# mLSTM heads: state steps and scores on the projections' PSUM tiles, the head's steps moved later, row sums later, Fourier stage in background steps

## The chip, the cores and the metric

One Trainium2 chip, one core of it. The time is device microseconds of one execution of the whole program. TensorE (PE) multiplies matrices into PSUM tiles, with its weight loads on a track of their own (PEld); VectorE (DVE) and ScalarE (ACT) read PSUM and work element by element; GpSimd (POOL) and SyncE (SP) mostly issue DMA transfers. Each engine works its instructions off in the order in which the compiled program holds them.

## The reference, cut to what matters

One layer of a diffusion backbone: 1024 latent tokens and 256 context tokens, 1024 channels, float32. Half a SwiGLU feed-forward, then token mixing (a 2-D Fourier transform of one channel group beside a bidirectional chunkwise mLSTM of 4 heads with 256 channels), then another half feed-forward.

```python
def ada_params(cvec, w, b):
    m = jax.nn.silu(cvec) @ w + b          # 9 x 1024 columns: shift, scale, gate of each sub-layer
...
    qk = jax.nn.silu(dwconv(p[..., COL_Q:COL_V], conv_w, conv_b))    # convolution over 3 tokens
...
# mLSTM, one direction, one chunk of 128 tokens
        w = jnp.exp(dmat - m_t[..., None])                            # decay inside the chunk
        s = jnp.einsum("bhtd,bhsd->bhts", qx, kx) * w                 # scores
        num = a[..., None] * jnp.einsum("bhtd,bhde->bhte", qx, C) + jnp.einsum("bhts,bhse->bhte", s, vx)
        den = a * jnp.einsum("bhtd,bhd->bht", qx, n) + jnp.sum(s, axis=-1)
        h = num / jnp.maximum(jnp.abs(den), jnp.exp(-m_t))[..., None]
        C_new = decay[..., None, None] * C + jnp.einsum("bhsd,bhse->bhde", kx * wk[..., None], vx)
...
        return h_f + flip(h_b)                                        # both directions
    y = jnp.fft.fftn(z, axes=(1, 2, 4), norm="ortho").real            # the Fourier half
```

## The kernel before

**Projections.** Every large matrix product goes through `mm3` (L153): three 128x512 matmuls, one each for the high and the low part of the split operands, so a projection of 128 output channels (`feat_major`) is 24 matmuls for each of the two halves of 512 tokens. The float32 weights `wr` come by DMA, ACT casts them to `wh` (L140) and DVE forms the rest `wl` (L141). Results go to PSUM tiles with the tag "mm" (4 of them). Small work uses two other PSUM tags: "aux" (4) and "qc" (for the products of q with the states).

**Background steps.** Code that must run beside the projections is written as Python generators. Before every three matmuls the projection calls `tick(1/16)`; `tick` adds `rate/16` to a credit, at most 8, and takes one step of the generator at the head of the queue for each whole credit (a second, separate generator, `side`, has its own rate). While no generator is queued the credit still grows, so a newly queued one starts with up to 8 steps at once. The compiled program's order within an engine is found by a scheduler after that and can differ from the order of the Python calls.

**A head.** For each of the 4 heads the program runs the projections of k (two of 128 channels, k0 and k1), then of q (q0, q1), then a few gate projections. `qk_proj` evicts each projection to a row with margins (ACT, L1259), and `conv` forms the convolution over three tokens and its SiLU (DVE L979, L980, L981, ACT L983, DVE L984), for each half of the tokens. `mlstm_head` runs as the background generator beside the q and gate projections:

- *State phase*, chunks 7 down to 1: `tokens` turns the k of a chunk from channel-major to token-major (PE transposes L1292 into an aux tile, ACT copy L1293), `state_keys` scales it (ACT, L1141), `state_step` multiplies with v into two aux tiles (L1149) and adds to the decayed state (DVE, L1154). All 8 backward states are kept.
- *Main loop*, chunks 0 to 7: `weights(c)` fetches the decay rows (DMA `m<-r_l`), adds the mask (DVE L1320), takes the exponential (ACT L1322), multiplies q by k into an aux tile `S` (L1325) and S by the decay (DVE L1328), multiplies q by the two states (L1334), advances the forward state (L1149, L1154) and forms the combined score matrix (DVE L1347, L1348). `turn(c)` transposes this (PE L1357, ACT L1358) one step later, `values(c)` multiplies it by v (L1364) and normalises (DVE L1368, which waits for POOL's part of the square root), `store(c)` transposes the result (L1375) and writes it out.

**Other work around it.** The row sums of the modulation (`ada_rest`): for one half of 1024 columns, eight DMAs of 128x512 into "ld" (or other) tiles, each multiplied and added by DVE (L251, L253) into an accumulator; ACT and DVE split it, PE sums over partitions with a selector matrix (L264), and `ada_cols` turns the row (L277). In the heads this is the `side` generator from head 1 on; the scheduler may set its instructions earlier. The Fourier stage `fourier_rest` is a plain call after q1 of head 0: its PE work (L1469, L1477) runs in one piece on mm tiles. `ctx_project` makes the keys and states of the context tokens before head 0, with the same `state_step`.

Of the kernel before, what the change touches and what calls it, by code (L numbers as in the profile page):

```python
# [13 lines left out]
ALU = mybir.AluOpType  # L14
# [20 lines left out]
class Kernel:  # L35
# [203 lines left out]
    def ada_rest(self, streams, chunks, tags=("wa", "u", "u", "b"), halves=(0, 1), lag=0):  # L239
        nc = self.nc  # L240
        w = self.a["w_ada"][0]
        for ch in chunks:
            for hf in halves:
                acc = {s: self.s512(tags[1]) for s in streams}
                for k in range(ND):
                    t = self.s512(tags[0])
                    nc.sync.dma_start(t, w[k * P : (k + 1) * P, ch * D + hf * TB : ch * D + (hf + 1) * TB])
                    yield
                    for s in streams:
# [5 lines left out]
                yield  # L255
                for s in streams:
                    ah, al = self.s512(tags[2], F32R), self.s512(tags[2], F32R)
                    self.split_act(ah, al, acc[s])
                    if s == streams[0]:
                        pr = self.aux()  # L260
                    for _ in range(1 + lag):
                        yield
                    for i, part in enumerate((ah, al)):
                        nc.tensor.matmul(pr[:2, :], self.sel[:, s, :], part, start=s == streams[0] and i == 0,  # L264
                                         stop=s == streams[-1] and i == 1)
# [602 lines left out]
    def ffn_ctx_in(self, w13, uh, ul):  # L868
# [3 lines left out]
        for c in range(6):  # L872
# [29 lines left out]
            self.defer(lambda gt=gt, n=wid // 256: self.ctx_turn(gt, n, g))  # L902
# [253 lines left out]
    def ctx_project(self, u, gw):  # L1156
# [14 lines left out]
        def key_in(f, c, raw):  # L1171
# [10 lines left out]
            self.defer(lambda: key_out(ct, kf), 2.0)  # L1182
# [9 lines left out]
        for c in range(2):  # L1192
# [7 lines left out]
            for f in range(4):  # L1200
                self.defer(lambda f=f, c=c, raw=raw: key_in(f, c, raw), 0.5 + f)
# [28 lines left out]
    def feat_major(self, col, u2, sink):  # L1230
# [3 lines left out]
        ps = [self.mm() for _ in range(NB)]  # L1234
        for b in range(NB):
            for k in range(ND):
# [34 lines left out]
    def mlstm_head(self, h, q, k, v, gates):  # L1271
# [25 lines left out]
        kw = {}  # L1297
        tokens(NCH - 1)
# [12 lines left out]
        work = {}  # L1311

        def weights(c):
            A, B = self.s512("m"), self.s512("m")
            W = A[:, :256].rearrange("p (d s) -> p d s", d=2)
            SW = A[:, 256:512].rearrange("p (d s) -> p d s", d=2)
# [6 lines left out]
            S = self.aux()  # L1323
            for i in range(2):
                nc.tensor.matmul(S[:, :P], at(q, i, c), at(k, i, c), start=i == 0, stop=i == 1)  # L1325
            den = self.small([P, 12], "den", bufs=3)
# [12 lines left out]
            if c < NCH - 1:  # L1339
                self.state_step(kw.pop(c), va(c), db[:, h, c : c + 1], Cf, Cf)  # L1340
# [4 lines left out]
            nc.vector.tensor_tensor(sc, rd, col2(1, c), op=ALU.mult)  # L1345
            pr = B[:, :P]
            nc.vector.tensor_scalar_mul(pr, SW[:, 1, :], rd[:, 1:2])  # L1347
            nc.vector.scalar_tensor_tensor(pr, SW[:, 0, :], rd[:, 0:1], pr, op0=ALU.mult, op1=ALU.add)  # L1348
            hh = B[:, 256:512]
            nc.scalar.activation(hh, qc[0][:, :DH], AF.Copy, scale=sc[:, 0:1])  # L1350
            nc.vector.scalar_tensor_tensor(hh, qc[1][:, :DH], sc[:, 1:2], hh, op0=ALU.mult, op1=ALU.add)
            work[c] = A, B, den

        def turn(c):
            A, B, den = work[c]
# [4 lines left out]
        def values(c):  # L1360
            A, B, den = work[c]
# [4 lines left out]
            nc.scalar.activation(A[:, :DH], hh, AF.Square, accum_out=den[:, 10:11])  # L1366
# [3 lines left out]
        def store(c):  # L1370
            A, B, den = work.pop(c)
# [54 lines left out]
    def fourier_rest(self):  # L1426
# [15 lines left out]
        pt = self.mm()  # L1442
# [5 lines left out]
        pt = self.mm()  # L1448
# [369 lines left out]
```

## Time and profile before

| | us |
|---|---|
| median of 3 runs | 2721.26 (2717.82 to 2724.28) |
| the profiled execution | 2721.47 |
| its span, first to last instruction | 2719.7 |
| PE busy | 2643.7 |
| DVE busy | 1858.5 |
| ACT busy | 1104.7 |

The profiled execution stands 0.21 us above the median, and 1.8 us lie outside its span. PE is busy for 97% of the span, so the time is that of PE's matmuls plus what PE waits. A busy PE is not yet a PE at its peak: matmuls overlap, each of the 128x512 ones is reported with about 0.40 us though the next starts 0.23 us later, so waits shorter than about 0.17 us do not show as idle, and a lowered clock shows as busy time too.

### The profile page before, as it was taken

What the parts mean: (1) busy time and instruction counts of PE and PEld (TensorE: products, weight loads), DVE (VectorE), ACT (ScalarE), POOL (GpSimd) and SP (SyncE); (2) the same over time, 40 slices, a digit from 0 to 9 for tenths busy, and PEclk for the clock granted to TensorE, in tenths of its full rate; (3) what the DMA queues carried; (4) which work ended last, traced back from release to release, by engine and by line L of the source; (5) the groups of instructions that cost most, each with busy time, mean ns of one, the idle gap of its engine ahead of it and who ended that gap; (6) DMA issues with size and microseconds to landing.
All of it is one profiled execution on the core that took longest, in us unless ns stands there. A gap on an engine that the chain in (4) does not pass through costs nothing.

```text
span 2719.7 us, 34141 instructions
## 1 busy us (share of the span) xinstructions
PE 2643.7 (97%) x11657; PEld 2109.1 (78%) x11657; DVE 1858.5 (68%) x3341; ACT 1104.7 (41%) x1893; POOL 194.9 (7%) x387
## 2 busy tenths in 40 slices
PE   8899999999999999999999999999999999999998
PEld 5778888777877777777878778778887888888876
DVE  5688787899678638565364675555667887865665
ACT  4543333454455436233243333433345433334542
POOL 1111010000000001000000000000001110111000
PEclk9999999999999999999999999999999999999999
DMA  9765454868578645325223443355556654537773
GB/s 299 243 199 173 151 178 153 276 216 289 153 225 255 197 135 173 104 68 156 83 78 105 129 125 103 104 156 191 177 160 203 188 171 151 168 116 258 252 248 139
DMA packets 408990, 472.53 MB, mean 174 GB/s; under 512 B 25497, under 2 KB 256450, under 8 KB 408816
## 3 DMA queue, kind: packets, MB, share of 16 engines
q1 hardware_dynamic: 393824, 423.96, 50.3%
q0 software_dynamic: 14848, 46.33, 4.5%
q8 instruction: 92, 1.51, 0.2%
q14 instruction: 82, 0.67, 0.1%
q10 hardware_dynamic: 144, 0.07, 0.0%
HBM read 373.21 MB, written 97.04 MB: 173 GB/s over the span
## 4 chain that ended last, share of the span: by engine, by line
PE 75%; DVE 9%; DMA 8%; issue 5%; ACT 2%; SPq 1%; POOL 0%; DVEq 0%; POOLq 0%; ACTq 0%
PE mm L153 68%; DMA m<-r_l 2%; PE aux L1149 2%; DMA wr<-in_w_a_dram 2%; PE qc L1334 1%; DVE wl L141 1%; DVE u L253 1%; DMA ld<-in_w_ada_dram 1%; DMA ld<-xT 1%; DVE g L146 1%; DMA u<-in_w_ada_dram 1%; PE mm L234 1%; DMA ld<-h 0%; ACT wh L140 0%; DVE wl L146 0%
## 5 line engine op out<-in xcount | busy, mean ns | idle before, releaser
L153 PE MATMUL mm<-g,wh 128*128 128x512 f32 (+1 forms) x2552 | 827.8, 404 | 4.9 <-ACT wh L145 2.8
L153 PEld LDWEIGHTS mm<-g,wh 128*128 128x128 f32 (+1 forms) x2552 | 477.4, 189 | 108.1 <-ACT wh L145 3.7
L153 PE MATMUL mm<-g,wl 128*128 128x512 f32 (+1 forms) x1276 | 505.7, 398 | 1.6 <-DVE wl L146 1.6
L153 PE MATMUL mm<-g,o 128*128 128x512 f32 x2112 | 497.6, 395 | 0.0
L153 PEld LDWEIGHTS mm<-g,o 128*128 128x128 f32 x2112 | 397.6, 188 | 93.0
L141 DVE TENSOR_TENSOR wl<-wr,wh 128x1024 fp32r<-128x1024 f32 x226 | 278.0, 1231 | 190.4 <-ACT wh L140 189.7
L140 ACT CAST wh<-wr 128x1024 fp32r<-128x1024 f32 x226 | 236.2, 1046 | 331.7 <-PE mm L153 274.8
L153 PE MATMUL mm<-wh,g 128*128 128x512 f32 x1032 | 332.6, 399 | 2.7 <-DVE rs_t L311 1.4
L153 PEld LDWEIGHTS mm<-g,wl 128*128 128x128 f32 (+1 forms) x1276 | 240.7, 189 | 55.5 <-DVE wl L146 3.5
L153 PE MATMUL mm<-u,wh 128*128 128x512 f32 (+1 forms) x848 | 269.5, 400 | 5.2 <-DVE m L706 3.5
L153 PEld LDWEIGHTS mm<-wh,g 128*128 128x128 f32 x1032 | 194.5, 188 | 49.7 <-DVE rs_t L311 1.8
L153 PE MATMUL mm<-wl,g 128*128 128x512 f32 x516 | 204.4, 396 | 0.0
L153 PEld LDWEIGHTS mm<-u,wh 128*128 128x128 f32 (+1 forms) x848 | 160.2, 191 | 44.2 <-DVE m L706 3.9
L153 PE MATMUL mm<-wh,u 128*128 128x512 f32 x544 | 179.5, 404 | 2.0 <-ACT wh L140 2.0
L153 PE MATMUL mm<-u,wl 128*128 128x512 f32 (+1 forms) x424 | 167.4, 398 | 2.8 <-DVE wl L141 2.7
L584 DVE TENSOR_TENSOR t<-mm,t 128x512 f32<-128x512 f32 x128 | 88.1, 688 | 77.2 <-PE mm L153 77.2
L146 DVE TENSOR_TENSOR g<-t,g 128x512 fp32r<-128x512 f32 x150 | 100.2, 688 | 35.1 <-ACT g L145 23.9
L153 PEld LDWEIGHTS mm<-wh,u 128*128 128x128 f32 x544 | 103.2, 190 | 24.8 <-ACT wh L140 2.4
L145 ACT CAST o<-wa 128x512 fp32r<-128x512 f32 x88 | 54.6, 621 | 160.0 <-PE mm L153 153.5
L145 ACT CAST wh<-wr 128x1024 fp32r<-128x1024 f32 (+1 forms) x72 | 62.6, 871 | 136.7 <-PE mm L153 75.8
L153 PEld LDWEIGHTS mm<-wl,g 128*128 128x128 f32 x516 | 97.3, 189 | 22.9 <-issue 0.7
L145 ACT CAST g<-t 128x512 fp32r<-128x512 f32 x150 | 88.5, 619 | 60.8 <-PE mm L153 39.3
(472 smaller groups left out, 3552.9 us busy)
## 6 DMA issues: line engine op xcount, KB each, us to landing
wr<-in_w_a_dram SPq DMA_DIRECT2D x124, 512.0 KB, 4.4
t<-gx SPq DMA_DIRECT2D x170, 256.0 KB, 3.9
wr<-in_w_in_dram SPq DMA_DIRECT2D x80, 512.0 KB, 3.8
wr<-in_w_b_dram SPq DMA_DIRECT2D x70, 512.0 KB, 4.7
gx<-m POOLq DMA_DIRECT2D x88, 256.0 KB, 3.8
gx<-t POOLq DMA_DIRECT2D x66, 256.0 KB, 3.9
ld<-in_w_ada_dram SPq DMA_DIRECT2D x64, 256.0 KB, 2.8
ld<-h SPq DMA_DIRECT2D x48, 256.0 KB, 3.9
```

The source lines that it names most:

```text
L140: nc.scalar.copy(hv, rv)
L141: nc.vector.tensor_tensor(lv, rv, hv.bitcast(F32), op=ALU.subtract)
L145: self.nc.scalar.copy(hi, src)
L146: self.nc.vector.tensor_tensor(lo, src, hi.bitcast(F32), op=ALU.subtract)
L153: mul = lambda x, y, start, stop: self.nc.tensor.matmul(out, x, y, start=start, stop=stop, skip_group_check=grown)
L234: nc.tensor.matmul(pt[:2, :], self.sc[:, k, :], t, start=k == 0, stop=k == ND - 1)
L253: nc.vector.scalar_tensor_tensor(acc[s], t, self.sc[:, k, s : s + 1], acc[s], op0=ALU.mult, op1=ALU.add)
L584: add = lambda o, x, y: nc.vector.tensor_tensor(o, x, y, op=ALU.add)
L1149: nc.tensor.matmul(pt[:, :257], kw[:, i * P : (i + 1) * P], vaug, start=True, stop=True)
L1334: nc.tensor.matmul(pt[:, :257], at(q, i, c), C[:, i * 257 : (i + 1) * 257], start=i == 0, stop=i == 1)
```

## The change

What it does, in the order of the diff:

1. `ada_rest`: sums of a half are put off by `lag` steps through a queue; both streams' sums come in one group of matmuls, after the next half has begun to load. In the feed-forward it uses four tags instead of "u" alone and lag 4; in the heads lag 3.
2. `state_step` uses mm tiles in place of aux tiles, in the heads and in `ctx_project`.
3. `feat_major` takes its second PSUM tile only when its second half begins.
4. `mlstm_head` begins with three empty steps. In the main loop the decay part of `weights` becomes `weigh`, run one chunk ahead; the scores become `scores`, with `S` in an mm tile; the forward state step comes a step after its scores; `turn` and `values` come one chunk after the scores, `store` two. The exponential's tile is freed after the scores, the "m" tag has 5 tiles in both.
5. `fourier_rest` becomes the `side` generator of head 0, with aux tiles and empty steps between its parts, and so runs beside the v, k and q projections of head 0.
6. The heads' rate is 5.6 in place of 5.0.

```diff
@@ -236,9 +236,26 @@
             nc.scalar.copy(row[:2, :], pt[:2, :])
             self.ada_cols(row, (0, 1), ch, 0)
 
-    def ada_rest(self, streams, chunks, tags=("wa", "u", "u", "b"), halves=(0, 1), lag=0):
+    def ada_rest(self, streams, chunks, tags=("wa", "u", "u", "b"), halves=(0, 1), lag=1):
+
         nc = self.nc
         w = self.a["w_ada"][0]
+        todo = deque()
+
+        def step():
+            for x in todo:
+                x[0] -= 1
+            while todo and todo[0][0] <= 0:
+                todo.popleft()[1]()
+
+        def sums(parts, ch, hf):
+            pr = self.aux()
+            for n, (s, part) in enumerate(parts):
+                nc.tensor.matmul(pr[:2, :], self.sel[:, s, :], part, start=n == 0, stop=n == len(parts) - 1)
+            row = self.s512(tags[3])
+            nc.scalar.copy(row[:2, :], pr[:2, :])
+            todo.append([lag, lambda: self.ada_cols(row, streams, ch, hf)])
+
         for ch in chunks:
             for hf in halves:
                 acc = {s: self.s512(tags[1]) for s in streams}
...
@@ -253,21 +271,17 @@
                             nc.vector.scalar_tensor_tensor(acc[s], t, self.sc[:, k, s : s + 1], acc[s],
                                                            op0=ALU.mult, op1=ALU.add)
                 yield
+                step()
+                parts = []
                 for s in streams:
                     ah, al = self.s512(tags[2], F32R), self.s512(tags[2], F32R)
                     self.split_act(ah, al, acc[s])
-                    if s == streams[0]:
-                        pr = self.aux()
-                    for _ in range(1 + lag):
-                        yield
-                    for i, part in enumerate((ah, al)):
-                        nc.tensor.matmul(pr[:2, :], self.sel[:, s, :], part, start=s == streams[0] and i == 0,
-                                         stop=s == streams[-1] and i == 1)
-                row = self.s512(tags[3])
-                nc.scalar.copy(row[:2, :], pr[:2, :])
-                for _ in range(1 + lag):
-                    yield
-                self.ada_cols(row, streams, ch, hf)
+                    parts += [(s, ah), (s, al)]
+                todo.append([lag, lambda parts=parts, ch=ch, hf=hf: sums(parts, ch, hf)])
+                del acc
+        while todo:
+            yield
+            step()
 
     def ada_cols(self, row, streams, ch, hf):
...
         for i in range(2):
-            pt = self.aux()
+            pt = self.mm()
             nc.tensor.matmul(pt[:, :257], kw[:, i * P : (i + 1) * P], vaug, start=True, stop=True)
...
         ww = self.wunit(w[:, :, col : col + P])
-        ps = [self.mm() for _ in range(NB)]
+        ps = []
         for b in range(NB):
+            ps.append(self.mm())
             for k in range(ND):
                 self.tick(1 / 16)
...
         kw = {}
+        for _ in range(3):
+            yield
         tokens(NCH - 1)
         yield
...
-        work = {}
-
-        def weights(c):
-            A, B = self.s512("m"), self.s512("m")
+        work, decay = {}, {}
+
+        def weigh(c):
+
+            A = decay[c] = self.s512("m")
             W = A[:, :256].rearrange("p (d s) -> p d s", d=2)
-            SW = A[:, 256:512].rearrange("p (d s) -> p d s", d=2)
             rv = rs.rearrange("(d h) t -> d h t", d=2)[:, h, c * P : (c + 1) * P]
             nc.sync.dma_start(W, rv.unsqueeze(0).to_broadcast([P, 2, P]))
             for d in range(2):
                 nc.vector.scalar_tensor_tensor(W[:, d, :], W[:, d, :], col(3, c, d), self.mask[:, d, :],
                                                op0=ALU.add, op1=ALU.add)
             nc.scalar.activation(A[:, :256], A[:, :256], AF.Exp)
-            S = self.aux()
+
+        def scores(c):
+            A, B = decay.pop(c), self.s512("m")
+            W = A[:, :256].rearrange("p (d s) -> p d s", d=2)
+            SW = A[:, 256:512].rearrange("p (d s) -> p d s", d=2)
+            S = self.mm()
             for i in range(2):
                 nc.tensor.matmul(S[:, :P], at(q, i, c), at(k, i, c), start=i == 0, stop=i == 1)
-            den = self.small([P, 12], "den", bufs=3)
+            den = self.small([P, 12], "den", bufs=4)
             for d in range(2):
                 nc.vector.scalar_tensor_tensor(SW[:, d, :], S[:, :P], 1.0, W[:, d, :], op0=ALU.mult, op1=ALU.mult,
                                                accum_out=den[:, d : d + 1])
...
+        weigh(0)
         while q[1] is None:
             yield
         kw[0] = self.state_keys(kt(0), col(0, 0, 0))
-        for c in range(NCH + 1):
+        for _ in range(2):
+            yield
+
+        for c in range(NCH + 2):
             if c < NCH:
-                weights(c)
+                scores(c)
                 yield
-                turn(c)
-            if c > 0:
-                store(c - 1)
-            yield
-            if c < NCH:
-                values(c)
+                if c < NCH - 1:
+                    self.state_step(kw.pop(c), va(c), db[:, h, c : c + 1], Cf, Cf)
+                if c + 1 < NCH:
+                    weigh(c + 1)
                 if c + 1 < NCH - 1:
                     kw[c + 1] = self.state_keys(kt(c + 1), col(0, c + 1, 0))
+            if 0 < c <= NCH:
+                turn(c - 1)
+            yield
+            if 0 < c <= NCH:
+                values(c - 1)
+            if c > 1:
+                store(c - 2)
+            if c < NCH:
                 yield
...
-        pt = self.mm()
+        for _ in range(2):
+            yield
...
-        self.later(self.load_x(a["ctx"][0], CTX, "c", xc, tag="u"), self.ada_rest([0, 1], [2, 3], "uuuu", lag=2),
+        self.later(self.load_x(a["ctx"][0], CTX, "c", xc, tag="u"), self.ada_rest([0, 1], [2, 3], ("wa", "u", "u", "b"), lag=4),
...
@@ -1711,11 +1749,15 @@
         v = None
         self.side_rate = 3.0
         for h in range(HEADS):
-            if h == 1:
-                self.side = self.ada_rest([0], [5, 6, 7, 8], ("ld", "acc", "rb", "b"), lag=1)
+            if h == 0:
+                self.side = self.fourier_rest()
+            elif h == 1:
+                for _ in self.side:
+                    pass
...
-            self.later(self.mlstm_head(h, q, k, v[h % 2], gates), rate=5.0)
+            self.later(self.mlstm_head(h, q, k, v[h % 2], gates), rate=5.6)
             for i in range(2):
                 q[i] = self.qk_proj(2 * h + i, u2)
-            self.rate = 5.0
-            if h == 0:
-                self.fourier_rest()
+            self.rate = 5.6
             for _ in range((len(todo) + HEADS - 1 - h) // (HEADS - h)):
                 fill()
             self.drain()
```

Three places show how it moves instructions. The first is PE at the start of head 1, from the last matmul of the projection k1 on: `u_2598` is the second half of k0, `u_2615` the second half of k1 after its convolution, `mm_2635`/`mm_2636` the first tile of q0. Before, with 28 further matmuls of q0 where the dots stand:

```order
L153 MATMUL mm_2620_11644<-g_1761_7642,wl_2618_11640 128x512
L1292 MATMUL aux_2640_11739<-ident_63,u_2598_11547 128x128
L1292 MATMUL aux_2641_11743<-ident_63,u_2598_11547 128x128
...
L153 MATMUL mm_2636_11733<-g_1763_7644,wh_2633_11728 128x512
L153 MATMUL mm_2636_11733<-g_1755_7636,wl_2634_11729 128x512
L1292 MATMUL aux_2640_11739<-ident_63,u_2615_11636 128x128
L1292 MATMUL aux_2641_11743<-ident_63,u_2615_11636 128x128
```

and in the changed kernel:

```order
L153 MATMUL mm_2621_11671<-g_1640_7069,wl_2618_11640 128x512
L1307 MATMUL aux_2639_11738<-ident_63,u_2598_11547 128x128
L1307 MATMUL aux_2640_11742<-ident_63,u_2598_11547 128x128
L1307 MATMUL aux_2639_11738<-ident_63,u_2615_11636 128x128
L1307 MATMUL aux_2640_11742<-ident_63,u_2615_11636 128x128
...
L1163 MATMUL mm_2646_11756<-u_2243_9660,kw_2641_11746 128x257
L1163 MATMUL mm_2647_11759<-u_2243_9660,kw_2641_11746 128x257
...
L1163 MATMUL mm_2657_11783<-u_2242_9659,kw_2649_11766 128x257
L1163 MATMUL mm_2658_11786<-u_2242_9659,kw_2649_11766 128x257
L153 MATMUL mm_2635_11732<-g_1691_7253,wh_2633_11728 128x512
```

The 30 matmuls of q0 that stood between the transposes of k0's half and those of k1's half now stand behind the transposes and the first three state steps. The same holds at the start of heads 0, 2 and 3 (in head 0 one state step stands ahead of q0 in place of three).

The second place is DVE at the start of head 0 in the changed kernel: the rows around the convolution of k1's second half (`wa_2372` and `wa_2373` are k1's two rows, `u_2366` the result).

```order
L1280 COPY wa_2372_10465<-wa_2373_10466 128x1
L271 SCALAR_TENSOR_TENSOR acc_2696_11947<-ld_2714_12042,sc_83,acc_2696_11947 128x512
L995 SCALAR_TENSOR_TENSOR t_2374_10473<-wa_2372_10465,cv_687,t_2374_10473 128x512
L271 SCALAR_TENSOR_TENSOR acc_2696_11947<-ld_2725_12097,sc_83,acc_2696_11947 128x512
L993 TENSOR_SCALAR t_2376_10480<-wa_2373_10466,cv_687 128x512
L998 SCALAR_TENSOR_TENSOR u_2365_10407<-t_2375_10477,t_2374_10473 128x512
L994 SCALAR_TENSOR_TENSOR t_2376_10480<-wa_2373_10466,cv_687,t_2376_10480 128x512
L995 SCALAR_TENSOR_TENSOR t_2376_10480<-wa_2373_10466,cv_687,t_2376_10480 128x512
L271 SCALAR_TENSOR_TENSOR acc_2696_11947<-ld_2731_12138,sc_83,acc_2696_11947 128x512
L998 SCALAR_TENSOR_TENSOR u_2366_10408<-t_2377_10484,t_2376_10480 128x512
```

In the kernel before, the same convolution holds no row of the row sums; the first 16 of them (two accumulators) stand there in the main loop of head 0, behind its first forward state steps. Now all 16 stand ahead of the first state step.

The third place is PE in the main loop of head 3, from chunk 1's scores (`S` is `aux_3329` before, `mm_3337` now) to the state step behind them. Before:

```order
L1325 MATMUL aux_3329_14950<-u_3215_14479,u_3288_14758 128x128
L1334 MATMUL qc_3332_14960<-o_3274_14667,u_3288_14758 128x257
L1149 MATMUL aux_3333_14964<-u_2869_12790,kw_3323_14924 128x257
L153 MATMUL mm_3309_14854<-g_1756_7637,wh_3306_14849 128x512
L153 MATMUL mm_3309_14854<-g_1764_7645,wh_3306_14849 128x512
L1149 MATMUL aux_3334_14967<-u_2869_12790,kw_3323_14924 128x257
```

and now; the first dots stand for products of q with the states, the second for 7 more projection matmuls:

```order
L1347 MATMUL mm_3337_14987<-u_3239_14550,u_3308_14818 128x128
...
L1356 MATMUL qc_3340_14997<-o_3295_14756,u_3308_14818 128x257
L153 MATMUL mm_3331_14954<-g_1639_7068,wh_3322_14900 128x512
...
L153 MATMUL mm_3346_15027<-g_1691_7253,wl_3345_15024 128x512
L1163 MATMUL mm_3347_15031<-u_2876_12812,kw_3335_14969 128x257
L1163 MATMUL mm_3348_15034<-u_2876_12812,kw_3335_14969 128x257
L1377 MATMUL aux_3351_15044<-ident_63,m_3326_14925 128x128
```

The state step stands 9 projection matmuls behind the scores in place of directly behind them, its tiles no longer follow `S` through the four aux tiles, and the transpose behind it is that of the chunk before (`m_3326`; chunk 1's own tile is `m_3336`).

More of the change, by code (lines that the diff above doesn't have):

```diff
@@ L1345, in weights @@
             nc.vector.tensor_tensor(sc, rd, col2(1, c), op=ALU.mult)
+            hh = B[:, 256:512]
+            nc.scalar.activation(hh, qc[0][:, :DH], AF.Copy, scale=sc[:, 0:1])
+            nc.vector.scalar_tensor_tensor(hh, qc[1][:, :DH], sc[:, 1:2], hh, op0=ALU.mult, op1=ALU.add)
             pr = B[:, :P]
@@ L1348, in weights @@
             nc.vector.scalar_tensor_tensor(pr, SW[:, 0, :], rd[:, 0:1], pr, op0=ALU.mult, op1=ALU.add)
[L1349 to L1352, printed above, removed]
+            work[c] = B, den
         def turn(c):
-            A, B, den = work[c]
+            B, den = work[c]
             pt = self.aux()
@@ L1360, in values @@
         def values(c):
-            A, B, den = work[c]
+            B, den = work[c]
             hh = B[:, 256:512]
@@ L1370, in store @@
         def store(c):
-            A, B, den = work.pop(c)
+            B, den = work.pop(c)
             hh = B[:, 256:512]
@@ L1441, in fourier_rest @@
         k32 = kr[:, :256].rearrange("p (a c) -> p a c", c=8)[:, :, 0]
-        pt = self.mm()
+        for _ in range(2):
+            yield
+        pt = self.aux()
         for g in range(4):
@@ L1447, in fourier_rest @@
                        pt[:, :P].rearrange("p (g i r) -> p g i r", g=4, i=2))
-        pt = self.mm()
+        for _ in range(2):
+            yield
+        pt = self.aux()
         for i in range(2):
@@ L1451, in fourier_rest @@
                              start=i == 0, stop=i == 1)
-        y32 = self.s512("wa")
+        y32 = self.small([P, 64], "y32", bufs=1)
         nc.scalar.copy(y32[:, :64], pt[:, :64])
@@ L1461, in fourier_rest @@
                 zz.append(t)
+            yield
             Y = [self.s512("acc"), self.s512("b")]
             for j2 in range(2):
-                pt = self.mm()
+                yield
+                pt = self.aux()
                 for jj in range(2):
@@ L1475, in fourier_rest @@
                         (nc.scalar.copy if i else nc.vector.tensor_copy)(dst[:, 2 * j2 + jj], pv[:, i, jj])
-            pp, pq = self.mm(), self.mm()
+            for _ in range(2):
+                yield
+            pp, pq = self.aux(), self.aux()
             nc.tensor.matmul(pp, kh[:, :P], Y[0], start=True, stop=True)
@@ L1655, in ctx_in @@
             yield from self.prenorm(self.reload(xc[0], CTX), xc[1:], CTX, 1, 0, uc)
-            yield from self.ada_rest([0, 1], [4], lag=2)
+            yield from self.ada_rest([0, 1], [4], lag=4)
         self.later(ctx_in(), rate=3.5)
@@ L1713, in run @@
         for h in range(HEADS):
-            if h == 1:
-                self.side = self.ada_rest([0], [5, 6, 7, 8], ("ld", "acc", "rb", "b"), lag=1)
+            if h == 0:
[3 more added lines that the diff above has]
+                    pass
+                self.side = self.ada_rest([0], [5, 6, 7, 8], ("ld", "acc", "rb", "b"), lag=3)
             if h % 2 == 0:
                 v = [[self.slot("u") for _ in range(4)] for _ in range(2)]
-                br = self.bias_row(C_V + h * DH)
+                br = self.bias_row(C_V + h * DH, "st")
                 for b in range(NB):
```

11 lines of the change are left out of this document (5 added, 6 removed).

## The prediction, made before the changed kernel was run

> **What bounds the kernel now.** I read the page first, then PE's waits, then the heads stretch by stretch, then the timeline of two places.
>
> ```profile
> PE 2643.7 (97%) x11657; PEld 2109.1 (78%) x11657; DVE 1858.5 (68%) x3341; ACT 1104.7 (41%) x1893; POOL 194.9 (7%) x387
> PE 75%; DVE 9%; DMA 8%; issue 5%; ACT 2%; SPq 1%; POOL 0%; DVEq 0%; POOLq 0%; ACTq 0%
> ```
>
> PE is busy 2643.7 of 2719.7 us, and the chain that ended last runs on PE for 75%. The change neither adds nor removes matmuls, so the time moves only with what PE waits and with its clock. At most 76 us of shown idle time can be won.
>
> ```profile
> PE aux L1149 <- DVE m L1328: 9.1, 6, 3.4
> PE aux L1357 <- DVE m L1348: 7.0, 5, 2.8
> PE aux L264 <- ACT u L145: 3.6, 2, 2.0
> PE aux L1375 <- DVE m L1368: 3.6, 4, 1.6
> PE mm L1477 <- DVE acc L1475: 1.3, 1, 1.3
> PE mm L1469 <- DMA ld<-z: 1.0, 3, 0.5
> ```
>
> These are PE's waits by line: total, times, longest. The heads' main loop has three: the state step waits for the scores' reader (9.1), the transposes `turn` and `store` for DVE (7.0 and 3.6): 19.7 us. Busy time by stretch agrees:
>
> ```profile
> core 0: us, PE busy (x) PEld busy (x) DVE busy (x) ACT busy (x) POOL busy (x), PEclk, DMA share, GB/s
> 500.00:710.00 210.00, 199.86 (x873) 157.69 (x873) 188.64 (x299) 97.21 (x162) 0.00 (x0) 0.99 0.75 246
> 1023.00:1089.00 66.00, 62.59 (x271) 47.42 (x271) 60.23 (x140) 44.12 (x69) 8.19 (x40) 0.97 0.59 170
> 1200.00:1234.00 34.00, 31.70 (x135) 22.45 (x133) 21.24 (x81) 10.84 (x33) 0.68 (x2) 1.00 0.42 129
> 1353.00:1373.00 20.00, 20.00 (x93) 14.48 (x92) 12.15 (x24) 10.12 (x21) 0.45 (x2) 1.00 0.10 27
> 1234.00:1319.00 85.00, 77.99 (x364) 63.81 (x363) 46.21 (x150) 26.97 (x67) 4.39 (x8) 1.00 0.48 139
> 1373.00:1475.00 102.00, 99.10 (x459) 81.26 (x458) 59.59 (x193) 38.02 (x88) 6.19 (x29) 0.98 0.36 102
> 1567.00:1668.00 101.00, 98.20 (x460) 80.07 (x459) 63.75 (x201) 37.58 (x89) 5.88 (x11) 1.00 0.40 112
> 1717.00:1821.00 104.00, 96.88 (x446) 78.14 (x445) 58.86 (x194) 41.04 (x94) 4.48 (x9) 0.98 0.45 130
> ```
>
> The last four rows are the main loops of heads 0 to 3: idle 7.0, 2.9, 2.8 and 7.1 us, 19.8 together. 1353 to 1373 is head 1's state phase: no idle time at all. 1200 to 1234 is the Fourier stage: 2.3 idle. 500 to 710 (context's feed-forward, with row sums) has 10.1 idle, 1023 to 1089 (context's keys and states) 3.4.
>
> **The change part by part.** *Main loop: gain.* The longest wait, in head 3:
>
> ```profile
> 1735.03 0.61 PE L1325 MATMUL aux<-u,u 128*128 128x128 f32 x4
> 1736.16 0.82 PE L153 MATMUL mm<-g,wh 128*128 128x512 f32 x2
> 1738.47 0.35 DVE L1320 SCALAR_TENSOR_TENSOR m<-m,cols_l,mask 128x128 f32<-128x128 f32 x1 [4.15 <-DMA m<-r_l]
> 1740.42 0.70 PE L1149 MATMUL aux<-u,kw 128*128 128x257 f32 x2 [3.44 <-DVE m L1328]
> ```
>
> The decay rows landed late, DVE's mask waited 4.15 us, the exponential and L1328 followed, and PE's second state matmul, whose aux tile holds `S` until then, waited 3.44. The change takes this apart: the decay is made a chunk ahead, the state step has mm tiles and 9 projection matmuls (9 x 0.23, the spacing of starts in the h1 rows below: 2.1 us) ahead of it, `turn` comes a chunk after its scores. What is late next is `values` behind `turn`, with again 9 matmuls over one ACT copy. I take 19 of 23 us: the 19.8 shown and some 3 in waits too short to show, less 4 that stay. Bounds: 12 (new waits on the shared mm tiles) to 23.
>
> *Fourier stage: gain.* Its 2.3 us of idle go when its pieces run among the v projection's matmuls, and about as much in the unshown gaps of 64 isolated small matmuls may stay or go; I take 3, from 1 to 5. Its DVE and ACT work stays and now runs beside the convolutions.
>
> *Start of each head: loss.* Here the order moved against the kernel. Head 1 before:
>
> ```profile
> 1353.40 0.40 PE L153 MATMUL mm<-g,wl 128*128 128x512 f32 x1
> 1353.60 1.05 ACT L140 CAST wh<-wr 128x1024 fp32r<-128x1024 f32 x1 [3.97 <-PE mm L153]
> 1353.63 0.38 PE L1292 MATMUL aux<-ident,u 128*128 128x128 f32 x2
> 1354.55 0.69 ACT L1259 ACTIVATE wa<-mm,cc 128x512 f32<-128x512 f32 x1
> 1354.68 1.23 DVE L141 TENSOR_TENSOR wl<-wr,wh 128x1024 fp32r<-128x1024 f32 x1 [3.66 <-ACT wh L140]
> 1356.00 0.75 DVE L981 SCALAR_TENSOR_TENSOR t<-wa,cv,t 128x512 f32<-128x512 f32 x1
> 1357.25 0.75 DVE L980 SCALAR_TENSOR_TENSOR t<-wa,cv,t 128x512 f32<-128x512 f32 x1
> 1359.96 0.69 DVE L984 SCALAR_TENSOR_TENSOR u<-t,t 128x512 f32<-128x512 f32 x1 [0.70 <-ACT t L983]
> 1360.74 0.41 PE L1292 MATMUL aux<-ident,u 128*128 128x128 f32 x2
> ```
>
> The last matmul of k1 starts at 1353.40. A cast that ACT began first, the eviction (L1259), DVE's weight rest (L141) and the convolution's operations follow, and its second half is written at 1360.65: 7.25 us. PE fills them with q0: between the transposes at 1353.63 and at 1360.74 lie 30 projection matmuls, 6.9 us. In the changed order these 30 stand behind the waiting transposes and the first state steps. The compiled order keeps the cast and L141 in the same places in the chain, so the cover is the last matmul's own 0.23 us and two transposes of the same kind, another 0.23: PE stands 7.25 - 0.46 = 6.8 us. The three empty steps do not help, because with 8 credits saved up they are spent at the first tick together with the five that follow. Heads 1 to 3: 3 x 6.8 = 20.4 us. Without the cast (0.95 us from end to end of it on ACT) the chain could not be under about 6.3, so the floor is 3 x 5.8 = 17.4.
>
> Behind the wait the first state steps run with little beside them: copy and scaling on ACT (0.33 and 0.52 us), then a pair of small matmuls per chunk. In head 1 before, the way from the transposes at 1360.74 to the first state matmul took 1.5 us, filled by projections; now it is bare, less the seven transposes now done there, so about 1 us per head is lost. Against this stands a row of PE's weight loads:
>
> ```profile
> PEld aux L1292 <- DVE o L1154: 5.4, 17, 0.3
> ```
>
> These 5.4 us (aux tiles that wait for the state's reader) go with four mm tiles and 9 matmuls between later steps. I set the two off to nothing, from -3 to +6.
>
> *Head 0: more loss.* There three additions of the row sums stand inside k1's convolution, and three just ahead. Their cost and pace in the trace before:
>
> ```profile
> 1242.78 0.75 DVE L253 SCALAR_TENSOR_TENSOR acc<-ld,sc,acc 128x512 f32<-128x512 f32 x1 [2.07 <-DMA ld<-in_w_ada_dram]
> 1250.44 0.74 DVE L253 SCALAR_TENSOR_TENSOR acc<-ld,sc,acc 128x512 f32<-128x512 f32 x1
> ```
>
> 0.75 us each, and from the first to the last of five of them 7.66 us, 1.9 apiece, since only two "ld" tiles take turns on the DMA. Three add 2.25 to the chain of 7.25 less 0.46: 9.0 us if the data are there. If DVE falls behind the DMA's pace, up to 3 x 1.2 more: 12.6. I take 9.0, the nearest row being the addition itself. All head starts: 29.4 us, from 24 to 34.
>
> *Clock: small loss.* After head 3's 3.44 us wait the clock dropped, and once in head 1:
>
> ```profile
> 1403.40:1406.80 3.40, 3.40 (x10) 2.63 (x9) 3.08 (x10) 0.47 (x1) 0.00 (x0) 0.52 0.53 142
> 1741.00:1745.00 4.00, 4.00 (x14) 3.19 (x13) 2.65 (x11) 1.42 (x4) 0.00 (x0) 0.57 0.51 159
> 1745.00:1749.00 4.00, 4.00 (x19) 3.31 (x18) 1.70 (x3) 2.92 (x8) 0.02 (x1) 1.00 0.11 33
> ```
>
> A granted clock of 0.57 over 4 us is 1.7 us of matmul time lost, 0.52 over 3.4 us 1.6. Four waits of 7 to 9 us, one drop each: +6.8; these two drops, behind waits of the main loop, go: -3.4. Sum +3.4, from 0 to +10. [...]
>
> *Row sums in the feed-forward, context's states: nothing.* The 3.6 us at L264 (sums waiting for the split) go with the lag, but in the compiled order some row transposes now follow ACT's copy with no matmul between, and waits of up to 2.0 (the longest of L264) come twice or so: 0, from -5 to +5. The context's state steps now run back to back, without projections between, and the next projection's tile queues behind them: +0, up to +3 (the stretch has 3.4 idle now).
>
> Sum against the profiled execution: 2721.5 + 29.4 + 3.4 - 19 - 3 = 2732.3 us. The median of the runs is 0.2 lower: **2732 us**, slower by 0.4%.
>
> **The rivals.**
>
> *Faster: the gains outrun short waits.* If the chain loses the cast and L141 lies beside it (5.8 per head, 7.5 in head 0: 25), one clock drop more than now (1.7), the main loop gives 23, Fourier 4, and the 10.1 idle us of 500 to 710 halve: 25 + 1.7 - 23 - 4 - 5 = -5; with the state phase's 3 more and 3 of context's, -11: 2710. For it: every one of these idle times is a row above. Against it: it needs all of them at once.
>
> *No change.* The waits come as I say, the clock does not fall further, and the main loop gives its full 23, Fourier 5: 29.4 - 28 = +1: 2723. For it: the two large terms are of one size. Against it: the mm tiles are now shared by projections, states and scores.
>
> *Much slower: DVE is late in head 0 and the clock stays down.* Head 0 at 12.6, two drops of clock per wait (+10 net), 12 won in the main loop because each mm tile now waits for DVE's L1328 or L1154, +5 in the row sums, refill +6: 33 + 10 - 12 - 2 + 11 = +40 at most; half of the excess gives 2748. It decides where DVE's in-order queue, 68% busy, is behind PE by more than the 2.1 us of cover. Against it: DVE's share in the main loops is 55 to 63%.
>
> **How the numbers follow.** Chances: forecast 0.49, faster 0.18, no change 0.19, much slower 0.14. The forecast's own range, from its terms' middle bounds, is 2724 to 2742. A measurement of this kernel tells about 0.2%, 5.4 us, from no change. Faster by more than that: 0.18; within: 0.19 and a small part of the forecast's low end, 0.22; slower: 0.60. The range for 8 in 10 reaches halfway into the faster case and over most of the much slower one: 2709 to 2750.
>
> **What would show each step.** Right: in PE's waits a new row of L1307 (token transposes) waiting for DVE L998, four times, 6.8 us each in heads 1 to 3 and 9 or more in head 0, about 29 in all; a granted clock near 0.5 right behind each; the rows of 9.1, 7.0 and 3.6 nearly gone; main loops with idle times of about 1 us each. Wrong: if that row is missing or its waits are under 4 us, the start of the heads was misread and the time should come out near 2705; if the waits are there and the time is still below 2716, the gains elsewhere were undersized; if L1377, L1384 or L1163 show waits of several us, the main loop's gain was oversized.

## The result

The changed kernel is slower: 2765.01 us (median of 4 runs, 2761.43 to 2767.18) against 2722.64 us; the ratio is 1.0155 with a 95% interval of 1.0139 to 1.0171. The direction was forecast, the size was not: +42 us in place of about +11.

Two lines from the head of the page of the profiled execution:

```profile
span 2763.9 us, 34229 instructions
PE 2653.4 (96%) x11657; PEld 2120.5 (77%) x11657; DVE 1864.4 (67%) x3341; ACT 1101.5 (40%) x1893; POOL 193.7 (7%) x387
```

The span grew by 44.2 us with the same number of matmuls on PE. Busy time grew by 9.7 us, which can only be matmuls at a lower clock (a row of four of L1163 took 2.05 us at a granted clock of 0.50, from 1383.70 on, and 1.03 at 1.00, from 1391.24 on) or spread apart; idle time by 34.5. The rows of PE's waits that the readings below use (total, times, longest; other rows stand between them):

```profile
PE aux L1307 <- DVE u L998: 28.2, 4, 8.1
PE mm L153 <- DVE wl L141: 8.2, 7, 4.0
PE mm L153 <- DVE g L146: 7.8, 4, 3.0
PE aux L1384 <- ACT m L1378: 5.3, 6, 1.6
PE mm L153 <- ACT wh L145: 4.9, 5, 1.7
PE aux L1146 <- ACT m L1129: 3.7, 1, 3.7
PE aux L1395 <- DVE m L1388: 2.6, 5, 1.1
PE aux L1395 <- ACT b L256: 2.4, 1, 2.4
PE aux L1377 <- DVE m L1385: 1.6, 2, 0.8
PE aux L1384 <- DVE ada_l L295: 1.5, 1, 1.5
```

The first row is the predicted one: the token transposes wait four times for the convolution, 28.2 us where 29 were forecast. The main loop's rows of before, 9.1, 7.0 and 3.6, have become 1.6 (L1377) and 2.6 (L1395), with the state step gone from the heads' rows. But three rows are new there: `values` (L1384) waits 5.3 for ACT's copy behind `turn`, and `store` and `values` wait 2.4 and 1.5 for readers in the row sums (L256, L295), which share the aux tiles with them. There are two aux tiles in both kernels (`bufs=2` in `aux`), not four as the text ahead of the prediction says. And four rows have nothing to do with the heads: projections that wait for their weights' preparation (L141, L146, L145) and the gate rows' transposes (L1146).

To see where the time went, each matmul's start was subtracted from the next one's in the trace, less the usual distance for its shape, and the excess summed by stage. It counts idle time, the short waits that busy time hides, and a lowered clock alike. Us lost in each stage that differs, and in the two ends, for the profiled executions of all kernels of this study, e1 to e8 as named below ("start" of a head: from its first token transpose to the last backward state step; the main loop of head 0 holds the Fourier stage before and in e5, 4.5 before):

```
stage                      before  after  e1    e2    e3    e4    e5    e6    e8    e7
first 500 us                 27.6   28.1  26.1  28.5  26.1  25.4  26.8  28.2  26.0  26.8
feed-forward, context        21.5   35.5  33.3  37.0  20.0  34.6  19.1  19.0  23.8  20.7
context's keys and states    10.6   15.5  20.7  13.0  15.4  15.9  17.1  16.2  17.2  11.1
start of head 0               1.3   10.7   1.4   1.8  12.4  10.6   9.9   1.1   0.8   1.0
start of head 1               1.3   10.4   0.2   1.3   9.3   9.9  10.0   0.2   0.2   0.2
start of head 2               1.2    9.8   0.1   1.1   9.7   9.9  12.4   0.1   0.1   0.2
start of head 3               1.3    9.3   0.2   1.3   9.3   9.6   9.7   0.1   0.2   0.2
main loop of head 0          12.9    4.8   1.2   7.2   4.7   5.5  15.1   1.4   0.9   0.7
main loop of head 1           5.6    9.3   8.5  12.8   8.4  12.0   6.1   8.0   7.0   6.2
main loop of head 2           4.4    1.8   1.1   2.4   1.8   1.4   2.8   1.1   1.1   1.2
main loop of head 3          10.8    3.6   4.9   6.8   4.4   3.8  11.5   5.1   6.1   5.9
after the heads              11.4   15.6  15.6  14.4  13.5  14.8  12.8  13.3  14.6  14.3
```

Before to after: head starts +35.1, feed-forward +14.0, context's states +4.9, main loops and Fourier -14.2, after the heads +4.2. The first and the last row have the same program in all kernels and differ by up to 4 us between them, so no difference of that size in one stage means anything by itself. In the context's row the change, e1 and e4 have the same program too, and they lose 15.5, 20.7 and 15.9.

Head 1's start, PE's timeline in the changed kernel (start, duration, instructions, idle time before and what ended it):

```profile
1374.91 0.38 PE L1307 MATMUL aux<-ident,u 128*128 128x128 f32 x2
1381.99 0.69 PE L1307 MATMUL aux<-ident,u 128*128 128x128 f32 x2 [6.69 <-DVE u L998]
1382.92 0.90 PE L1307 MATMUL aux<-ident,u 128*128 128x128 f32 x3 [0.25 <-ACT g L1308]
1383.70 2.05 PE L1163 MATMUL mm<-u,kw 128*128 128x257 f32 x4
1385.54 0.42 PE L1307 MATMUL aux<-ident,u 128*128 128x128 f32 x1
1385.76 1.92 PE L1163 MATMUL mm<-u,kw 128*128 128x257 f32 x4
1387.47 0.64 PE L1307 MATMUL aux<-ident,u 128*128 128x128 f32 x2
1387.89 1.22 PE L1163 MATMUL mm<-u,kw 128*128 128x257 f32 x4
1388.76 0.81 PE L153 MATMUL mm<-g,wh 128*128 128x512 f32 x2
```

6.69 us of shown idle time where 6.8 were forecast. What was seen only in part is the stretch behind it: the first projection matmul starts 6.8 us after the wait has ended. The busy shares and the granted clock (PEclk) in windows of 1 us, five of them, show that the small matmuls there ran at half clock:

```profile
core 0: us, PE busy (x) PEld busy (x) DVE busy (x) ACT busy (x) POOL busy (x), PEclk, DMA share, GB/s
1377.00:1378.00 1.00, 0.00 (x0) 0.00 (x0) 0.96 (x4) 0.00 (x0) 0.00 (x0) 1.00 0.00 0
1378.00:1379.00 1.00, 0.00 (x0) 0.00 (x0) 0.96 (x3) 0.63 (x1) 0.35 (x1) 0.51 0.54 106
1382.00:1383.00 1.00, 0.75 (x3) 0.35 (x4) 0.00 (x0) 0.50 (x2) 0.00 (x0) 0.50 0.00 0
1387.00:1388.00 1.00, 1.00 (x5) 0.76 (x4) 0.63 (x2) 0.23 (x1) 0.00 (x0) 0.50 0.00 0
1388.00:1389.00 1.00, 1.00 (x6) 0.86 (x6) 0.48 (x2) 0.54 (x2) 0.00 (x0) 0.87 0.00 0
```

The clock fell to half 2.7 us into the wait and stayed there for 10.2 us, until just before the first projection matmul. By the clock records of the same trace it was at half for 10.24 us in heads 0 and 1 and for 6.83 us in heads 2 and 3; of this, 4.2, 6.3, 5.2 and 4.2 us (heads 0 to 3) lay behind the end of the wait, where PE had work.

### The profile page after: what moved, and what is told of

The parts are those of the page before. It is cut to its first block, busy times and chain, and to the rows that moved or that the text cites. A ratio compares the mean times of both kernels' runs of the same rounds, so it can differ in the third digit from the quotient of the medians.

```text
span 2763.9 us, 34229 instructions
## 1 busy us (share of the span) xinstructions
PE 2653.4 (96%) x11657; PEld 2120.5 (77%) x11657; DVE 1864.4 (67%) x3341; ACT 1101.5 (40%) x1893; POOL 193.7 (7%) x387
## 4 chain that ended last, share of the span: by engine, by line
PE 75%; DVE 10%; DMA 9%; issue 3%; ACT 2%; POOL 0%; SPq 0%; DVEq 0%; POOLq 0%; ACTq 0%
PE mm L153 67%; DMA m<-r_l 2%; PE mm L1163 2%; DMA wa<-in_w_ada_dram 1%; DVE wl L141 1%; PE qc L1356 1%; DMA ld<-h 1%; DVE g L146 1%; DVE u L271 1%; ACT wh L140 1%; DMA ld<-xT 1%; PE mm L234 1%; PE aux L1505 0%; DVE b L423 0%; DMA hn<-m 0%
## 5 line engine op out<-in xcount | busy, mean ns | idle before, releaser
L153 PEld LDWEIGHTS mm<-g,wh 128*128 128x128 f32 (+1 forms) x2552 | 475.4, 189 | 123.5 <-DVE g L146 11.2
L141 DVE TENSOR_TENSOR wl<-wr,wh 128x1024 fp32r<-128x1024 f32 x226 | 278.1, 1231 | 199.6 <-ACT wh L140 198.9
L146 DVE TENSOR_TENSOR g<-t,g 128x512 fp32r<-128x512 f32 x150 | 100.4, 686 | 34.8 <-ACT g L145 25.7
L145 ACT CAST o<-wa 128x512 fp32r<-128x512 f32 x88 | 54.6, 621 | 163.2 <-PE mm L153 156.2
L145 ACT CAST wh<-wr 128x1024 fp32r<-128x1024 f32 (+1 forms) x72 | 62.7, 871 | 126.7 <-PE mm L153 58.8
L145 ACT CAST g<-t 128x512 fp32r<-128x512 f32 x150 | 89.2, 619 | 54.5 <-PE mm L153 39.7
```

The costliest lines, as they stand in the source:

```text
L141: nc.vector.tensor_tensor(lv, rv, hv.bitcast(F32), op=ALU.subtract)
L145: self.nc.scalar.copy(hi, src)
L146: self.nc.vector.tensor_tensor(lo, src, hi.bitcast(F32), op=ALU.subtract)
L153: mul = lambda x, y, start, stop: self.nc.tensor.matmul(out, x, y, start=start, stop=stop, skip_group_check=grown)
```

## The experiments

My theory after the result had two parts. First, the heads' loss is the bare start: the wait for the convolution and the state steps behind it at half clock, moved there by the state step's tag alone. Second, the feed-forward's loss is the density of the row sums. The rival to the first was that the deeper main loop on shared mm tiles is itself at fault and the waits would come back there; the rival to the second that the "wa" tiles or the merged groups of sums cost the time. The expectations name each.

**e1: spend no saved credit at the head's start.** One line behind the queueing of a head:

```diff
             self.later(self.mlstm_head(h, q, k, v[h % 2], gates), rate=5.6)
+            self.credit = 0.0
```

> The changed kernel with one line more: the credit is set to zero when a head is queued, so that its three empty steps pass at the projection's own pace. In the compiled order 33 matmuls of q0 (7.6 us at 0.23 us) then stand between the end of k1 and the first token transposes in every head. Theory (the loss of the heads is the bare wait for the convolution of 7.25 us and the first state steps behind it, at half clock): the four waits of 28.2 us go but for 1 to 3 us in head 0, whose convolution takes about 9 us; the head starts cost about 1 to 2 us each in place of 9 to 11, -30 to -36 us in all: 2730 to 2736 us. Rival (the heads lose by the shared PSUM tiles of the main loop, and the waits only come later): the time stays above 2750 us with new waits in the main loop.

2721.65 us, ratio 0.9998 (0.9986 to 1.0010) to the kernel before: 43 us less than the change. PE's waits from 1200 to 1900 us:

```profile
PE aux L1395 <- DVE m L1388: 3.7, 5, 1.8
PE aux L1384 <- ACT m L1378: 2.7, 3, 1.4
PE aux L291 <- DVE m L1385: 2.7, 1, 2.7
PE aux L1307 <- DVE u L998: 1.1, 1, 1.1
```

Of 28.2 us at L1307 1.1 are left, in head 0. The starts lose 1.9 us in place of 40.2, and the main loops 15.7 in place of 19.5: nothing came back there. The rival falls. The gain was larger than expected (-43, not -30 to -36): the starts give 38.3 and now lose less than before the change (5.1), and the main loops give 3.8 more, which is no more than the table's scatter.

**e2: the state step back on aux tiles,** all else as changed:

```diff
         for i in range(2):
-            pt = self.mm()
+            pt = self.aux()
             nc.tensor.matmul(pt[:, :257], kw[:, i * P : (i + 1) * P], vaug, start=True, stop=True)
```

> The changed kernel with the state step back on aux tiles, everything else kept. In the compiled order 30 matmuls of q0 (37 in head 0) again stand between the transposes of k0's half and those of k1's. Theory (the tag of the state step alone moved the head's start): head starts back to about 1.5 us each, -34 us; the context's projections mixed with state steps again, -6 us; 2723 to 2732 us, and no return of the state step's waits in the main loop, since S stays in an mm tile. Rival (the state step's tag is needed in the main loop): 5 to 9 us of waits of L1163 in the main loop, 2735 to 2740 us.

2737.32 us, ratio 1.0052 (1.0031 to 1.0072). The starts come back as the theory says (5.5 in all), the context's stage by half (13.0). But the main loops lose 29.2 us, as many as before the change (29.2 without Fourier):

```profile
PE aux L1377 <- DVE st L1168: 11.6, 6, 3.3
PE aux L1395 <- DVE m L1388: 2.8, 5, 1.2
PE aux L1377 <- DVE m L1385: 2.1, 2, 1.7
```

So the rival held in part, under another name than it gave: it is not L1163 that waits but `turn`, whose aux tile is now the one that the state step's reader holds. In the changed loop the mm tiles for the state step keep `turn` from waiting; at the start of the head they make the loss.

**e5: the kernel before with that one edit,** aux to mm in `state_step` and nothing else:

```diff
         for i in range(2):
-            pt = self.aux()
+            pt = self.mm()
             nc.tensor.matmul(pt[:, :257], kw[:, i * P : (i + 1) * P], vaug, start=True, stop=True)
```

> The kernel before with one part of the change alone: the state step's tiles from mm in place of aux. In the compiled order no matmul of q0 stands any longer between k0's transposes and k1's, and several state steps follow bare. Theory (this tag alone moves the heads' starts, and with them the loss): token transposes wait for the convolution four times, 6.8 us each or more, the four starts lose 35 to 45 us and the context's stage 2 to 5; the main loop gains some of its 9.1 us of state-step waits; 2745 to 2765 us. Rival (the loss needs the empty steps, the lazily taken tiles or the deeper main loop as well): 2715 to 2730 us.

2764.87 us, ratio 1.0160 (1.0131 to 1.0188): as slow as the whole change.

```profile
PE aux L1292 <- DVE u L984: 28.7, 4, 8.7
PE aux L1357 <- DVE m L1348: 13.5, 10, 3.5
PE mm L1149 <- DVE o L1013: 5.2, 3, 3.2
```

Three lines tell the case: the four waits at the token transposes are there (28.7) with neither empty steps nor a deeper loop; the state step's wait of 9.1 has moved on to the transpose of the scores (7.0 before, 13.5 now), since without the deeper loop something else is just as late; and the context's state steps wait in their bare row. The head starts lose 42.0 us in place of 5.1, and the context's stage 6.5 more than before. That the total equals the change's is chance: here the feed-forward loses no more than before (19.1), and the main loops with the Fourier stage lose 35.5 in place of the change's 19.5. So the tag alone does not make the main loop better; it takes the deeper loop too. Why the scheduler keeps q0's matmuls behind the state steps when both use the mm tag was not tried apart.

**e3: the old pace for the feed-forward's row sums.** The change's row sums take 9 steps per half (eight loads and one more), where the old ones took 18 with two streams, at the same rate of steps. Nine empty ones more:

```diff
                 todo.append([lag, lambda parts=parts, ch=ch, hf=hf: sums(parts, ch, hf)])
                 del acc
+                for _ in range(9 if len(streams) == 2 else 0):
+                    yield
+                    step()
```

> The changed kernel with nine more empty steps per half in the row sums of the feed-forward, 18 in all as before. Theory (the new row sums take 9 steps per half in place of 18 and so ask for twice the DVE time per us in a stretch in which DVE is 90% busy; DVE's weight preparations come late): the 14.4 us lost between 514 and 890 us go, 2748 to 2754 us, and the additions spread to 690 us or later again. Rival (the two wa tiles that take the loads in place of u tiles, or the sums of both streams in one group, cause it): 2761 us or more.

2746.5 us, ratio 1.0084 (1.0063 to 1.0105): 18.5 us less than the change, of which the feed-forward's stage gives 15.5. DVE's time in the additions of the row sums alone, by stretch; before:

```profile
540.00:570.00 30.00, 9.55 (x14) 0.94 0.63 200
630.00:660.00 30.00, 0.26 (x1) 1.00 0.89 287
660.00:690.00 30.00, 12.39 (x18) 1.00 0.74 239
```

the change:

```profile
540.00:570.00 30.00, 13.52 (x20) 0.83 0.75 233
630.00:660.00 30.00, 14.10 (x21) 0.94 0.82 267
660.00:690.00 30.00, 0.56 (x1) 1.00 0.77 253
```

and e3:

```profile
540.00:570.00 30.00, 10.43 (x15) 1.00 0.70 216
630.00:660.00 30.00, 1.41 (x2) 0.94 0.90 299
660.00:690.00 30.00, 13.95 (x20) 1.00 0.78 247
```

The additions are the same 57 us in all. In the change 13.52 us of them fall between 540 and 570 and 14.10 between 630 and 660, and DVE is busy for 29.32 of the 30 us from 540 to 570 (28.27 before). Density alone is not enough, though: e3 has 13.95 us of them from 660 to 690, and PE is busy for 29.87 us there. It matters what stands behind the additions in DVE's queue. At 538 to 543 in the change, the rows of this chain:

```profile
538.12 0.62 ACT L145 CAST wh<-g 128x512 fp32r<-128x512 f32 x1 [1.94 <-DVE g L743]
538.22 2.87 DVE L271 SCALAR_TENSOR_TENSOR u<-wa,sc,u 128x512 f32<-128x512 f32 x4 [0.20 <-DMA wa<-in_w_ada_dram]
541.01 0.69 DVE L743 TENSOR_TENSOR g<-g,g 128x512 f32<-128x512 f32 x1
541.61 0.69 DVE L146 TENSOR_TENSOR wl<-g,wh 128x512 fp32r<-128x512 f32 x1
542.22 0.68 DVE L146 TENSOR_TENSOR g<-t,g 128x512 fp32r<-128x512 f32 x1
542.96 0.80 PE L153 MATMUL mm<-g,wh 128*128 128x512 f32 x1 [2.98 <-DVE g L146]
```

ACT's cast is done at 538.74, but four additions and a product (L743) stand ahead of the weight preparation (L146) in DVE's queue, and PE waits 2.98 us for it. e3 keeps the "wa" tiles and the merged sums and loses 20.0 in this stage (21.5 before the change), so the rival falls: it is the pace.

**e4: `turn(c-1)` ahead of `scores(c)`,** so that ACT copies the transposed scores before it scales the next chunk's products:

```diff
+            if 0 < c <= NCH:
+                turn(c - 1)
             if c < NCH:
                 scores(c)
...
-            if 0 < c <= NCH:
-                turn(c - 1)
             yield
```

> The changed kernel with turn(c-1) put ahead of scores(c), so that ACT's copy of the transposed scores stands ahead of ACT's scaling of the next chunk's products, which waits for DVE. Theory (the main loop's remaining waits are this copy in ACT's in-order queue): the 5.3 us of L1384 waiting for L1378 go to under 1.5, 2757 to 2762 us. Rival (the copy is late for other reasons, casts of weights, or turn now waits for DVE itself): L1377 waits for L1385 instead, 2763 to 2770 us.

2770.26 us, ratio 1.0184 (1.0156 to 1.0212): no gain. The runs of this kernel (2764.62 to 2778.39) and of the change overlap, so a loss is not shown either. In the heads' stretch:

```profile
PE aux L1377 <- DVE m L1385: 7.6, 5, 3.2
PE aux L1384 <- ACT m L1378: 0.7, 1, 0.7
```

The 5.3 us at L1384 went to 0.7, as the theory says, and came back as 7.6 at L1377, since `turn` now waits for the DVE operation that finishes `values` of the chunk before, its aux tile's reader. The rival's result came; it named the right rows.

**e6: both repairs,** e1's and e3's edits in one kernel.

> The changed kernel with both repairs: the credit set to zero when a head is queued, and nine more empty steps per half in the feed-forward's row sums. Theory (two separate losses): their gains add, -43 and -18 us from 2765: 2701 to 2707 us, below the kernel before. Rival (both free the same resource, or the one's gain depends on the other's loss): 2712 us or more.

2704.8 us, ratio 0.9936 (0.9913 to 0.9959) to the kernel before, 60 us less than the change: 43 and 18.5 add up. The two losses are separate, and without them the change is a gain of 0.6%.

**e8 and e7: the context's stage.** The change also lengthened three delays of the context's deferred steps, which the list ahead of the prediction leaves out. e8 is e6 with the delays of the context's deferred steps as they were (1.0, 2.0 and 0.5 + f in place of 1.5, 2.5 and 1 + f); e7 is e8 with the context's state steps on aux tiles, the heads' on mm:

```diff
-            pt = self.mm()
+            pt = (tile or self.mm)()
...
-                            C if n % 2 else None, N)
+                            C if n % 2 else None, N, self.aux)
```

> The run with both repairs, and the context's deferred steps back at the delays of the kernel before (1.0, 2.0 and 0.5 + f). Theory (the context's stage loses 3.5 us because PE stands 3.9 us at the transposes of the gate rows, which the later steps no longer cover): that wait falls to about 0.5 us, -3 to -5 us against the run with both repairs. Rival (the wait comes from the state steps on mm tiles): no change.

> As the run before it, and the context's state steps back on aux tiles (the heads' stay on mm tiles). Theory: the bare row of state steps at the end of the context's stage is filled with projections again, another -2 to -4 us; rival (aux tiles only move the wait): no change.

e8: 2703.93 us, ratio 0.9938 (0.9916 to 0.9960), nothing against e6. The wait at the gate rows' transposes fell from 3.7 to 0.4 us, but the state steps' wait for v rose from 1.5 to 5.2:

```profile
PE mm L1166 <- DVE o L1030: 5.2, 3, 3.2
```

e7: 2697.48 us, ratio 0.9914 (0.9887 to 0.9942), with neither wait in its list; the context's stage loses 11.1 us in place of 17.2, about as before the change (10.6). The rows fit the reading that the delays and the tag each bring one of the two waits (e5, with the tag alone, has the 5.2 too), so that undoing one only moves the loss. This is likely and not shown: the runs of e8 (2700.83 to 2709.52) and e7 (2691.98 to 2704.33) overlap, and the stage differs by 5.2 us between the change and e1, where its program is the same. e7 has the lowest median of this study, 24 us below the kernel before, timed beside it.

## Why the prediction was right, and where it was wrong

*Start of each head, 29.4 us.* Right in mechanism and size: 28.2 us shown, 6.69 in head 1 against 6.8, 8.1 at most (head 0) against 9.0. e1 and e5 show the cause from both sides.

*Behind the wait, "set off to nothing, from -3 to +6", and the clock.* Right in size, in part by luck. The starts lose 35.1 us more than before, about 7 beyond the waits, and the forecast had put 6.8 there for four drops of the clock: 29.4 + 6.8 = 36.2. But it meant one drop of about 3.4 us behind each wait. The trace shows half clock from within the wait on, for 6.83 to 10.24 us, of which 4.2 to 6.3 fell on work. How much of the 7 us is the clock and how much the bare order, no run separates. The 5.4 us of weight loads that waited for the state's reader (PEld L1292) are gone in the change, as forecast. Of the two drops that were to go from the main loops, both went and a new one of 3.41 us came (at 1480.41).

*Main loop, 19 us; Fourier stage, 3 us.* The main loops lost 29.2 us by the distances of starts and lose 19.5: a gain of 9.7, clock included, where the forecast has 19 and 3.4 for the clock, and below the lower bound of 12. This step failed. The shown waits fell from 19.7 us to 13.4, not to 4. The largest of those left (5.3) is "`values` behind `turn`, with again 9 matmuls over one ACT copy": the copy is one short operation, but ACT had been given the next chunk's scaling ahead of it, which waits for DVE's chain of small operations. Another 3.9 us (2.4 and 1.5) are waits for readers in the row sums on the two aux tiles, which no term had. The timeline of the changed kernel at head 0's longest wait for the copy:

```profile
1333.30 0.47 ACT L1367 ACTIVATE m<-qc,den 128x256 f32<-128x256 f32 x1 [2.90 <-DVE den L1365]
1333.67 0.26 ACT L1378 COPY m<-aux 128x128 f32<-128x128 f32 x1
1333.98 0.70 PE L1384 MATMUL aux<-u,m 128*128 128x256 f32 x2 [1.62 <-ACT m L1378]
```

ACT stands idle 2.90 us for the scaling, with the 0.26 us copy behind it, and PE waits 1.62. e4 removes this wait and wins nothing, so what the copy costs by itself stays open. The Fourier stage's 4.5 are gone from head 0's main loop, inside the bounds. With the start covered (e1) the main loops lose 15.7.

*Row sums in the feed-forward, "0, from -5 to +5".* The step that failed by the most: +14.0, and e3 takes 15.5 away. I looked at the waits at L264 and at the lag, and did not count how many steps a half takes: half as many at the same rate ask for the same additions in half the time, where the row for 500 to 710, quoted in the prediction, shows DVE busy for 188.64 of 210 us.

*Context's states, "+0, up to +3".* +4.9, over the bound but no more than this stage's scatter. e8 and e7 suggest that delays and tag cause it together, and do not show it.

*The sum.* Profile against profile the change cost 44.2 us, and the forecast was 10.8. By the table, the 33 us between are the feed-forward (14.0), the main loops with the Fourier stage and their two drops (25.4 forecast, 14.2 won: 11.2), the context's states (4.9) and the stretch after the heads (4.2), less 1.1 at the starts. After the heads the program is the same; PE's waits for DVE's weight rest (L141) are 2.3 us longer there (3.4 against 1.1) and one stretch at half clock is 6.83 us long in place of 3.41. Why is open.

*Rivals.* The nearest was "much slower", at 2748 and at most 40 us above the kernel before. Its point, DVE's queue behind PE, was right for the feed-forward and not for head 0, where it stood. Its two drops per wait came nearer to the 6.83 to 10.24 us of half clock than the forecast's one. Of the signs named, the row of L1307 came as described, and so did a wait of several us at L1384, the sign of an oversized gain in the main loop.

## What to carry to other kernels

A tile's tag is part of the schedule: giving a background step the projections' PSUM tiles helped, with the deeper loop, against its waits in one place and took away the filler in another, so read the compiled order on both sides of every wait, and at the start of a phase above all. When a background generator is rewritten, count its steps: fewer steps at the same rate is a heavier load per us on the engine it uses, and where that engine is 90% busy (here DVE, for 188.64 of 210 us before the change) the projections pay (here 14.0 us). Empty steps meant as a delay do nothing if saved-up credit is spent on them at once.

## What the runs showed of the hardware

In head 1 of the change the granted clock dropped 2.7 us into a wait (1.00 at 1377, 0.51 at 1378, with PE idle from 1375.3) and stayed at 0.50 up to 1388, also where PE was reported busy for the whole us with small matmuls (1387). A reported busy share of 1.00 is thus no sign that the clock is back.

By the clock records of the two profiled executions, without the first 20 and the last 12 us of each, the kernel before was at half clock nine times, for 3.41 us each, 30.7 us in all; the changed kernel was so eight times for 3.41 us, four times for 6.83 and twice for 10.24, 75.1 us in all. At the four starts of the heads in the change these stretches begin at 1214.17, 1378.02, 1586.23 and 1736.41. In head 1 PE was busy for 0.20 of the 3.42 us ahead of the drop (1374.60 to 1378.02), and in the three thirds of the 10.24 us behind it for 0.00, 0.76 and 1.00 of the time. What brought the clock back was not shown.

Waits of one length cost different times at half clock. In heads 1, 2 and 3 of the change PE waits 6.69, 6.70 and 6.69 us for the convolution; the clock drops 2.7, 5.0 and 4.1 us into the wait and is at half for 10.24, 6.83 and 6.83 us, of which 6.3, 5.2 and 4.2 us lie behind the wait; these starts lose 10.4, 9.8 and 9.3 us. What sets the difference was not shown. In the context's stage the waits add up to 8.0 us in the change and 7.9 in e1, but half clock to 6.8 and 17.1 us, and the stage loses 15.5 and 20.7.
